# A narrower second token tile, chosen by a branch, in the experts of a hybrid attention and mixture-of-experts block

## The chip, the cores and the metric

The kernel runs on one core of one Trainium2 chip. The metric is device time of one execution in microseconds (us), the median of several runs; smaller is better. PE is the matrix engine, PEld its weight-load port, ACT the scalar engine, DVE the vector engine, POOL the general engine that issues the indexed transfers, SP the queue that issues plain ones.

## The reference

One encoder block over 1024 tokens of width 1024: a dilated and a two-dimensional neighbourhood attention, then a mixture of 16 experts in 4 groups, then a last normalisation. The change touches the experts alone:

```
g_idx  = top-1 group of each token             (4 groups)
e_idx  = top-2 experts inside that group       (4 experts each)
combine[token, expert] = softmax(two logits) * group weight
gate = x @ w_gate[e]      # 1024 -> 256
up   = x @ w_up[e]        # 1024 -> 256
act  = silu(gate) * up * combine[:, e]
out += act @ w_down[e]    # 256 -> 1024
```

The routing depends on the data. On the inputs of the reference the experts, in the order in which the kernel takes them, get 118, 118, 124, 137, 117, 132, 134, 205, 128, 59, 87, 172, 75, 99, 147 and 196 tokens. They are called e0 to e15 below. The products run in a split form: each float32 operand is a high part and a low part, and a product is the sum of high by high, high by low and low by high.

## The kernel before

The attention takes the first 624 us or so. The experts follow, in one loop over e0 to e13 (L1494 to L1553); e14 and e15 come in a tail after it.

For each expert the lists of its token numbers lie in `gi`. `gather` (L1357, an indexed transfer issued by POOL) brings up to 128 token rows into a tile `xg`. `tokens_in` (L1395) turns the tile by eight transposes on PE into two tiles, `x_hi` (written by ACT) and `x_lo` (written by DVE). `expert_up` (L1406) does 24 products of 128x512 into one PSUM bank: for each of 8 slices of the width `x_hi` by `g_hi`, `x_hi` by `g_lo`, `x_lo` by `g_hi`, where the 512 columns are gate and up side by side. ACT takes Silu of the gate half, DVE multiplies by the up half and by the token's weight into `act`. `act_in` (L1419) turns and splits `act`; `expert_down` (L1428) does 6 products for each half `z` of the 1024 outputs, and ACT evicts them into `ye`. `scatter` (L1455, an indexed transfer that adds into `acc_d` in device memory) puts `ye` back. In the rows a scatter with the index `idx` is that of an expert's last tile; one with the index `gi` is that of a first tile whose expert has a second one.

The down products of an expert run one turn of the loop later, among the gate and up products of the next, so that PE always has work. `split_up` and `split_down` split the next experts' weights in quarters on ACT (`g_hi`, `d_hi`) and DVE (`g_lo`, `d_lo`) between those.

An expert with more than 128 tokens has a second tile, gathered into `xg1`. Its work stands under a branch at L1527, which the four engines PE, ACT, DVE and POOL each take by a register loaded by `counts` (L1380) from the counts in `n_i`. In the branch stand, for the second tile, `tokens_in`, `expert_up`, and then the whole down step of the *first* tile (`expert_down` twice, into the PSUM tag `s`), its eviction into `y1` and its scatter; the second tile's own down step then takes the place of the first one's in the next turn. So with these counts the branch is taken at e3, e5, e6, e7 and e11, and jumped over at the nine others. An engine that jumps over it still does a wait for its own work and raises the semaphores that the branch would have raised; on POOL one such instruction is `INC_SWDGE_SEM`, for the indexed transfer's semaphore.

What sets the order: each engine runs its own instructions in the order of the code. The tile pools decide the waits: `ye` has two buffers, so an eviction into `ye` waits for the scatter of two evictions earlier to have landed. All scatters add into one tensor `acc_d`, and each waits for the landing of the one before it. The branch's own `ye` (L1531) is taken inside the branch.

Of the kernel before, what the change touches and what calls it, by code (L numbers as in the profile page):

```python
# [9 lines left out]
F32 = mybir.dt.float32  # L10
# [62 lines left out]
def build(nc, tc, a, ctx, dbg=None):  # L73
# [874 lines left out]
    pk = rt.tile([128, 2, 8], F32, name="pk")  # L948
    feat = rt.tile([128, 2, 8, 6, 16], BF, name="feat")
    C = rt.tile([128, 8, 16], BF, name="C")  # L950
    n_i = rt.tile([128, 17], I32, name="n_i")
    place = small[:, 0:32].rearrange("p (t e) -> p t e", t=8)
    token = small[:, 32:56].rearrange("p (t k) -> p t k", t=8)

# [398 lines left out]
    def at(e):  # L1353
        return slice(ORDER[e], ORDER[e] + 1)

    def gather(x, idx, src=hn_d):
        return nc.gpsimd.indirect_dma_start(out=x, out_offset=None, in_=src[:, :],  # L1357
                                            in_offset=bass.IndirectOffsetOnAxis(ap=idx, axis=0), bounds_check=1023,
                                            oob_is_err=False)

    def new_x(name="xg"):
        return ex.tile([128, 1024], F32, name=name, bufs=2)

    g_l = ex.tile([128, 1024], F32, name="g_l", bufs=1)
    bcast_row(g_l, a["norm_final_g"], 1024)
    x0 = {}
    for e in range(2):
        x0[e] = new_x()
        gather(x0[e], gi[:, 0, at(e)])

    cnt = pos[:, 16 * (8 - LAST):16 * (9 - LAST)]
    V.tensor_copy(n_i[:, 0:16], cnt)
    nmax = rt.tile([128, 1], F32, name="nmax")
    V.tensor_reduce(nmax, cnt, axis=X, op=ALU.max)
    V.tensor_copy(n_i[:, 16:17], nmax)
    ET = mybir.EngineType
    engines = (ET.PE, ET.Activation, ET.DVE, ET.Pool)

    def counts(c0, c1, which):
        return nc.values_load_multi_w_load_instructions(  # L1380
            n_i[0:1, c0:c1], engines=which, min_val=0, max_val=1024,
            skip_runtime_bounds_check_because="a count of tokens lies in 0..1024")[1]

    weights()
    n_val = counts(0, 16, engines)
    V.tensor_tensor(down0[1][:, 0], raw[:, 0], f(down0[0][:, 0]), op=ALU.subtract)
    down_raw[2] = load_down(2)
    up_raw[3] = [load_up(3, z) for z in range(2)]
# [6 lines left out]
    def tokens_in(x):  # L1395
        xh = ex.tile([128, 8, 128], F32R, name="x_hi")
        xl = ex.tile([128, 8, 128], F32R, name="x_lo")
        for q in range(2):
            pt = bank("pt")
            for k in range(4):  # L1400
                nc.tensor.transpose(pt[:, k * 128:(k + 1) * 128], x[:, (4 * q + k) * 128:(4 * q + k + 1) * 128],  # L1401
                                    ident)
            split(xh[:, 4 * q:4 * q + 4, :], xl[:, 4 * q:4 * q + 4, :], pt.rearrange("p (k t) -> p k t", k=4))
        return xh, xl

    def expert_up(xs, W, wcol, act):  # L1406
        gh, gl = W[0], W[1]
        xh, xl = xs
        ps = bank("mm")
        i = 0  # L1410
        for k in range(8):
            for l, wt in ((xh, gh), (xh, gl), (xl, gh)):
                nc.tensor.matmul(ps, l[:, k, :], wt[:, k, :], start=i == 0, stop=i == 23)  # L1413
                i += 1
        sg = ex.tile([128, 256], F32, name="sg", bufs=1)
        nc.scalar.activation(sg, ps[:, 0:256], AF.Silu)
        V.scalar_tensor_tensor(act, ps[:, 256:512], wcol, sg, op0=ALU.mult, op1=ALU.mult)

    def act_in(act):  # L1419
        pt = bank("s")  # L1420
        for k in range(2):
            nc.tensor.transpose(pt[:, k * 128:(k + 1) * 128], act[:, k * 128:(k + 1) * 128], ident)
        ah = ex.tile([128, 256], F32R, name="a_hi")
        al = ex.tile([128, 256], F32R, name="a_lo")
        split(ah, al, pt[:, 0:256])
        return ah, al

    def expert_down(aa, W, z, y=None, tag="o"):  # L1428

        ah, al = aa  # L1430
        dh, dl = W[2], W[3]
        c = slice(512 * z, 512 * z + 512)
        ps = bank(tag)
        i = 0
        for k in range(2):
            kk = slice(k * 128, (k + 1) * 128)
            for l, wt in ((ah, dh), (ah, dl), (al, dh)):
                nc.tensor.matmul(ps, l[:, kk], wt[:, k, c], start=i == 0, stop=i == 5)  # L1438
                i += 1
        if y is not None:  # L1440
            nc.scalar.activation(y[:, c], ps, AF.Copy)  # L1441
        return ps

    def new_y():
        return ex.tile([128, 1024], F32, name="ye", bufs=2)
# [2 lines left out]
        return ex.tile([128, 256], F32, name="act", bufs=2)  # L1448

    def second_gather(e):  # L1450
        x1[e] = new_x("xg1")
        gather(x1[e], gi[:, 1, at(e)])

    def scatter(d, idx, src, **kw):
# [13 lines left out]

    x1, xs, waiting, added = {}, {}, [], []
    spacer = ex.tile([128, 2], F32, name="spacer", bufs=1)[:, 0:1]

    def add_rows():
# [27 lines left out]
    for e in range(14):  # L1502
        if e:
            xs[e + 1] = tokens_in(x0.pop(e + 1))
            if e + 3 < 16:
                x0[e + 3] = new_x()
                gather(x0[e + 3], gi[:, 0, at(e + 3)])
        add_rows()
        if last:
            aa, before, y = act_in(last[0]), last, new_y()  # L1510
            W[e] = W[e] + split_down(down_raw.pop(e))
            down_raw[e + 2] = load_down(e + 2)
            W[e + 1], quarter = split_up(up_raw.pop(e + 1), (e + 1) % 2)
            for q in range(3):
                quarter(q)
        act = new_act()
        idx = ex.tile([128, 1], I32, name="idx", bufs=4)
        expert_up(xs.pop(e), W[e], ws[:, 0, at(e)], act)
        rows = [gi[:, q, at(e)] for q in range(2)]
        nc.gpsimd.tensor_copy(idx, rows[0])  # L1520
        if not last:
            xs[1] = tokens_in(x0.pop(1))
            x0[3] = new_x()
            gather(x0[3], gi[:, 0, at(3)])
        if last:
            expert_down(aa, W[e - 1], 0, y)
        with tc.If(n_val[ORDER[e]] > 128):  # L1527
            xs1 = tokens_in(x1.pop(e))
            aa1 = act_in(act)
            expert_up(xs1, W[e], ws[:, 1, at(e)], act)  # L1530
            y1 = new_y()  # L1531
            for z in range(2):
                expert_down(aa1, W[e], z, y1, tag="s")
            added.append((e, scatter(acc_d, rows[0], y1, compute_op=ALU.add)))
            nc.gpsimd.tensor_copy(idx, rows[1])
        if e:
            quarter(3)
        if 0 < e < 13:
            up_raw[e + 3] = [load_up(e + 3, z) for z in range(2)]
        if last:  # L1540
            expert_down(aa, W.pop(e - 1), 1, y)
            waiting.append((before[2], before[1], y))
        if e == 13:
            add_rows()
        if e + 2 < 14:
            second_gather(e + 2)
        elif e == 12:
            x1[e + 2] = new_x("xg1")
            gather(x1[e + 2], gi[:, 1, at(e + 2)])
        last = act, idx, e  # L1550
        if e == 2:
            kept_rows()
            n_top, = counts(16, 17, mybir.ALL_ENGINES)  # L1553
# [266 lines left out]
```

## Time and profile before

| | us |
|---|---|
| median of 3 runs | 895.49 (895.33 to 896.38) |
| the profiled execution, its own time | 894.3 |
| its span in the trace | 892.5 |
| PE busy in the span | 834.3 (93%) |
| PEld busy | 695.0 (78%) |
| DVE busy | 565.1 (63%) |
| ACT busy | 512.6 (57%) |
| POOL busy | 234.4 (26%) |

The mean granted clock of PE is 0.977 of full speed. The profiled execution's own time exceeds its span by 1.8 us, and lies 1.2 us under the median. The shares are means over the whole program; the stage of the experts runs from about 624 us to the end, and has other limits than the attention before it.

### The profile page before, as it was taken

To read this page: it belongs to the slowest core of one execution; us is meant where nothing else is said; L and a number is where in the kernel's file an instruction comes from. 1 tells how busy PE (TensorE), PEld (TensorE's weight loads), DVE (VectorE), ACT (ScalarE), POOL (GpSimd) and SP (SyncE) were. 2 spreads that over 40 slices of the span, in tenths; PEclk is the share of its full clock that TensorE was granted. 3 is DMA by queue.
4 is the path that set the end of the run, shared out by engine and by line. 5 is a ranking of instruction groups with operands and counts; after the bars stand their busy time and mean duration, and the time that the engine had idled before them with its cause. 6 is when DMAs were issued, how large, how long until landed. Compare 5 with 4: busy or idle time off the path is not lost. (4 is left out here: it accounts for less than half of the span.)

```text
span 892.5 us, 13330 instructions
## 1 busy us (share of the span) xinstructions
PE 834.3 (93%) x4492; PEld 695.0 (78%) x4492; DVE 565.1 (63%) x1255; ACT 512.6 (57%) x1082; POOL 234.4 (26%) x187
## 2 busy tenths in 40 slices
PE   8999999999999999999898999999799999999962
PEld 5888878979889888878787887887677877777741
DVE  4551126776767767666677754677786566858693
ACT  5441127757667576677576623543585665857652
POOL 4001122221232202332310100000443343734553
PEclk8999999999999999999999999998999999999985
DMA  6865452314344141534447747995798987999743
GB/s 238 278 217 162 126 160 65 100 52 108 94 138 105 53 138 48 148 103 117 79 157 206 254 154 248 360 323 213 250 317 248 293 233 226 361 299 304 217 180 129
DMA packets 129919, 167.30 MB, mean 187 GB/s; under 512 B 15222, under 2 KB 101750, under 8 KB 129824
## 3 DMA queue, kind: packets, MB, share of 16 engines
q1 hardware_dynamic: 119616, 142.53, 49.6%
q0 software_dynamic: 10224, 23.79, 9.8%
q8 instruction: 41, 0.67, 0.3%
q14 instruction: 38, 0.31, 0.1%
HBM read 129.93 MB, written 47.47 MB: 199 GB/s over the span
## 5 line engine op out<-in xcount | busy, mean ns | idle before, releaser
L103 ACT ACTIVATE pt_hi<-ps_pt 128x512 fp32r<-128x512 f32 (+2 forms) x128 | 67.6, 528 | 70.6 <-PE ps_pt L509 41.5
L378 PE MATMUL ps_mm<-xhi,w_lo 128*128 128x512 f32 x256 | 105.1, 411 | 1.1 <-POOL w_lo L104 1.1
L378 PE MATMUL ps_mm<-xlo,w_hi 128*128 128x512 f32 x256 | 105.0, 410 | 0.0
L378 PE MATMUL ps_mm<-xhi,w_hi 128*128 128x512 f32 x256 | 102.9, 403 | 0.0
L104 POOL TENSOR_TENSOR w_lo<-w_raw,w_hi 128x1024 fp32r<-128x1024 f32 x16 | 38.3, 2394 | 229.3 <-ACT w_hi L103 229.3
L104 DVE TENSOR_TENSOR pt_lo<-ps_pt,pt_hi 128x512 fp32r<-128x512 f32 (+2 forms) x128 | 77.2, 603 | 31.8 <-ACT pt_hi L103 31.2
L424 DVE CUSTOM_DVE_ANT_0 p<-ps_s,bias 128x256 f32<-128x256 f32 (+1 forms) x192 | 81.8, 450 | 18.2 <-PE ps_s L411 10.8
L104 DVE TENSOR_TENSOR g_lo<-raw_up,g_hi 128x1024 fp32r<-128x1024 f32 x64 | 75.4, 1220 | 24.6 <-ACT g_hi L103 24.6
L1413 PE MATMUL ps_mm<-g_hi,x_hi 128*128 128x512 f32 x184 | 75.4, 410 | 0.9 <-ACT x_hi L103 0.9
L1413 PE MATMUL ps_mm<-g_hi,x_lo 128*128 128x512 f32 x184 | 74.0, 402 | 1.8 <-DVE x_lo L104 1.8
L1357 POOL DMA_INDIRECT xg<-hn_d,gi x32 | 44.3, 1383 | 118.0 <-ACT ge L1078 81.7
L1413 PE MATMUL ps_mm<-g_lo,x_hi 128*128 128x512 f32 x184 | 73.3, 398 | 0.0
L430 ACT ACTIVATE p<-p,stats 128x256 f32<-128x256 f32 x128 | 63.7, 500 | 9.7 <-DVE stats L424 9.5
L103 ACT ACTIVATE g_hi<-raw_up 128x1024 fp32r<-128x1024 f32 x64 | 64.3, 1067 | 0.9
L411 PE MATMUL ps_s<-k_hh,q_s 128*128 128x256 f32 (+1 forms) x192 | 60.7, 324 | 4.3 <-DMA k_hh<-k_hh 1.7
L411 PE MATMUL ps_s<-k_low,q_s 128*128 128x256 f32 (+1 forms) x192 | 62.6, 334 | 0.0
L411 PEld LDWEIGHTS ps_s<-k_hh,q_s 128*128 128x128 f32 x192 | 44.6, 232 | 11.2 <-DVE q_s L402 2.6
L378 PEld LDWEIGHTS ps_mm<-xhi,w_lo 128*128 128x128 f32 x256 | 48.7, 190 | 5.2 <-POOL w_lo L104 1.4
L378 PEld LDWEIGHTS ps_mm<-xhi,w_hi 128*128 128x128 f32 x256 | 48.7, 190 | 3.2
L378 PEld LDWEIGHTS ps_mm<-xlo,w_hi 128*128 128x128 f32 x256 | 48.5, 189 | 3.5
L411 PEld LDWEIGHTS ps_s<-k_low,q_s 128*128 128x128 f32 x192 | 44.7, 233 | 3.5
L430 ACT ACTIVATE p<-p,nm 128x384 f32<-128x384 f32 (+1 forms) x64 | 37.5, 586 | 14.4 <-DVE nm L424 14.0
(307 smaller groups left out, 2152.8 us busy)
## 6 DMA issues: line engine op xcount, KB each, us to landing
raw_up<-in_w_gate SPq DMA_DIRECT2D x32, 512.0 KB
raw_up<-in_w_up SPq DMA_DIRECT2D x32, 512.0 KB
raw_down<-in_w_down SPq DMA_DIRECT2D x16, 1024.0 KB
w_raw<-in_w_in SPq DMA_DIRECT2D x16, 512.0 KB
xt<-in_x SPq DMA_DIRECT2D x8, 512.0 KB
k_hh<-in_w_in SPq DMA_DIRECT2D x8, 512.0 KB
va_d<-vt SPq DMA_DIRECT2D x16, 256.0 KB
vb_d<-vt SPq DMA_DIRECT2D x8, 512.0 KB
```

Of the source, the lines that this page charges most:

```text
L103: nc.scalar.activation(hi, src, AF.Copy)
L104: (nc.gpsimd if pool else nc.vector).tensor_tensor(lo, src, f(hi), op=ALU.subtract)
L378: nc.tensor.matmul(ps, l[:, k, :], x[half][:, k, :], start=i == 0, stop=i == 23)
L411: nc.tensor.matmul(ps, self.q[h][:, qs], keys(k[h]), start=n == 0, stop=n == 1)
L424: nc.vector.tensor_tensor_reduce(out=p, in0=ps, in1=bias, scale=-0.125, scalar=3.0e38, op0=ALU.add, op1=ALU.min, accum_out=nm)
L430: nc.scalar.activation(p, p, AF.Exp, bias=nm, scale=-1.0, accum_out=l)
L1357: return nc.gpsimd.indirect_dma_start(out=x, out_offset=None, in_=src[:, :], in_offset=bass.IndirectOffsetOnAxis(ap=idx, axis=0), bounds_c ...
L1413: nc.tensor.matmul(ps, l[:, k, :], wt[:, k, :], start=i == 0, stop=i == 23)
```

## The change

The `If` on more than 128 tokens becomes two in a row. The first, on more than 192 tokens, holds the old body. The second, on 129 to 192 tokens (a second tile of 1 to 64 tokens), holds the same steps with `few_tokens_in` and `few_up`. `few_tokens_in` writes the high parts of 64 tokens into columns 0 to 63 of one tile `x_hi`, and the low parts into columns 64 to 127. `few_up` then needs 16 products (this tile by `g_hi` and by `g_lo`, 8 slices each) where `expert_up` has 24; the result's rows 64 to 127 hold the low parts' share. ACT copies these rows into the spent token tile (`room`), DVE adds the two halves, and Silu and the weighting follow on 64 rows.

Around it: `n_i` gets 16 more columns, with two more DVE operations that fill them (the flag "129 to 192 tokens"); four engines load 16 more registers from them (`n_few`); `x0` of two experts and `x1` of two experts are cleared on POOL before they are first gathered into; `x1` of the first two is taken earlier; and `y1` is taken ahead of both branches.

```diff
-    n_i = rt.tile([128, 17], I32, name="n_i")
+    n_i = rt.tile([128, 33], I32, name="n_i")
...
-    x0 = {}
+
+    x0, x1 = {}, {}
     for e in range(2):
         x0[e] = new_x()
+        nc.gpsimd.memset(x0[e], 0.0)
+    for e in range(2):
         gather(x0[e], gi[:, 0, at(e)])
+    for e in range(2):
+        x1[e] = new_x("xg1")
+        nc.gpsimd.memset(x1[e], 0.0)
...
     V.tensor_copy(n_i[:, 16:17], nmax)
+
+    few = rt.tile([128, 16], F32, name="few")
+    V.tensor_scalar(few, cnt, 128.5, None, op0=ALU.is_gt)
+    V.scalar_tensor_tensor(n_i[:, 17:33], cnt, 192.5, few, op0=ALU.is_lt, op1=ALU.mult)
...
     n_val = counts(0, 16, engines)
+    n_few = counts(17, 33, engines)
...
+    def few_tokens_in(x):
+        xx = ex.tile([128, 8, 128], F32R, name="x_hi")
+        for q in range(2):
+            pt = bank("pt")
+            for k in range(4):
+                nc.tensor.transpose(pt[:, k * 128:(k + 1) * 128], x[:, (4 * q + k) * 128:(4 * q + k + 1) * 128],
+                                    ident)
+            ks = slice(4 * q, 4 * q + 4)
+            split(xx[:, ks, 0:64], xx[:, ks, 64:128], pt.rearrange("p (k t) -> p k t", k=4)[:, :, 0:64])
+        return xx, x
+
+    def few_up(xs, W, wcol, act):
+        xx, room = xs
+        ps = bank("mm")
+        i = 0
+        for k in range(8):
+            for wt in W[0:2]:
+                nc.tensor.matmul(ps, xx[:, k, :], wt[:, k, :], start=i == 0, stop=i == 15)
+                i += 1
+        few = slice(0, 64)
+        nc.scalar.activation(room[few, 0:512], ps[64:128, :], AF.Copy)
+        V.tensor_tensor(room[few, 512:1024], ps[few, :], room[few, 0:512], op=ALU.add)
+        sg = ex.tile([128, 256], F32, name="sg", bufs=1)
+        nc.scalar.activation(sg[few], room[few, 512:768], AF.Silu)
+        V.scalar_tensor_tensor(act[few], room[few, 768:1024], wcol[few], sg[few], op0=ALU.mult, op1=ALU.mult)
...
-        with tc.If(n_val[ORDER[e]] > 128):
-            xs1 = tokens_in(x1.pop(e))
-            aa1 = act_in(act)
-            expert_up(xs1, W[e], ws[:, 1, at(e)], act)
-            y1 = new_y()
-            for z in range(2):
-                expert_down(aa1, W[e], z, y1, tag="s")
-            added.append((e, scatter(acc_d, rows[0], y1, compute_op=ALU.add)))
-            nc.gpsimd.tensor_copy(idx, rows[1])
+        x, y1 = x1.pop(e), new_y()
+        for cond, tokens, up in ((n_val[ORDER[e]] > 192, tokens_in, expert_up),
+                                 (n_few[ORDER[e]] > 0, few_tokens_in, few_up)):
+            with tc.If(cond):
+                xs1 = tokens(x)
+                aa1 = act_in(act)
+                up(xs1, W[e], ws[:, 1, at(e)], act)
+                for z in range(2):
+                    expert_down(aa1, W[e], z, y1, tag="s")
+                added.append((e, scatter(acc_d, rows[0], y1, compute_op=ALU.add)))
+                nc.gpsimd.tensor_copy(idx, rows[1])
```

How the instructions stand on the engines shows in three places. The first is DVE where the counts become registers, just ahead of the first expert (`feat`, `part` belong to the routing, `d_lo` is the low part of the first down weights):

```order
 L1093 TENSOR_TENSOR feat<-ev,wb 128x8x48 x2
-L1380 TENSOR_LOAD n_i
-L1386 TENSOR_TENSOR d_lo<-raw_down,d_hi 128x1024
+L1390 TENSOR_LOAD n_i x2
+L1397 TENSOR_TENSOR d_lo<-raw_down,d_hi 128x1024
 L1144 COPY part<-ps_o 128x32
 L1145 TENSOR_TENSOR part<-part,ps_o 128x32
```

A second register load stands ahead of the low parts.

The second place is POOL around an expert's branch in the loop. Before (the instruction ISA is the `INC_SWDGE_SEM` of a branch that is jumped over; names such as Pool_49 are semaphores):

```order
L1520 COPY idx<-gi 128x1
L1527 COMPARE_AND_BRANCH
L1455 DMA acc_d<-ye,gi 1024x1024 [waits DMASW4_49,Activation_49]
L1535 COPY idx<-gi 128x1 [waits Pool_49]
L1527 UNCONDITIONAL_BRANCH
L1527 ISA [waits Pool_49,DMASW5_49]
L1527 UNCONDITIONAL_BRANCH
L1357 DMA xg_7927<-hn_d,gi 128x1024 [waits DMASW6_49,PE_49]
L1357 DMA xg<-hn_d,gi 128x1024 [waits DMASW7_49,PE_49]
L1455 DMA acc_d<-ye,idx 1024x1024 [waits DMASW4_49,DMASW5_49,Activation_49,Pool_49]
```

The same place after, from the first branch's jumped-over part on:

```order
L1569 ISA [waits Pool_49,DMASW6_49]
L1569 UNCONDITIONAL_BRANCH
L1569 COMPARE_AND_BRANCH
L1494 DMA acc_d<-ye,gi 1024x1024 [waits DMASW6_49,DMASW7_49,DMASW5_49,Activation_49]
L1576 COPY idx<-gi 128x1 [waits Pool_49]
L1569 UNCONDITIONAL_BRANCH
L1569 ISA [waits Pool_49,DMASW7_49]
L1569 UNCONDITIONAL_BRANCH
L1357 DMA xg_8181<-hn_d,gi 128x1024 [waits DVE_49,DMASW6_49,PE_49,Activation_49]
L1357 DMA xg<-hn_d,gi 128x1024 [waits DMASW7_49,PE_49]
L1494 DMA acc_d<-ye,idx 1024x1024 [waits DMASW6_49,DMASW5_49,DMASW7_49,Activation_49,Pool_49]
```

Each expert has two such branches in a row, each with its own copy of the jumped-over part, and the gather into `xg1` waits for DVE and ACT too, which now read and write that tile.

The third place is PE in the branch. Before, from the branch to the first products:

```order
L1527 COMPARE_AND_BRANCH
L1401 MATMUL ps_pt<-ident,xg_6711 128x128 x8
L1422 MATMUL ps_s<-ident,act 128x128 x2
L1413 MATMUL ps_mm<-g_hi,x_hi 128x512
L1413 MATMUL ps_mm<-g_lo,x_hi 128x512
L1413 MATMUL ps_mm<-g_hi,x_lo 128x512
```

In the narrow branch after:

```order
L1569 COMPARE_AND_BRANCH
L1436 MATMUL ps_pt<-ident,xg_7937 128x128 x8
L1460 MATMUL ps_s<-ident,act 128x128 x2
L1448 MATMUL ps_mm<-g_hi,x_hi 128x512
L1448 MATMUL ps_mm<-g_lo,x_hi 128x512
```

The product with `x_lo` is gone from each of the 8 slices.

## Rows read from the trace of the kernel before

**Rows 1.** Busy time by engine, e5's stretch (us, busy and count each, clock, DMA, GB/s).
```profile
692.00:712.00 20.00, 19.86 (x97) 15.92 (x96) 11.00 (x14) 11.61 (x20) 5.40 (x5) 1.00 0.97 317
```

**Rows 2.** Timeline of PE in e5's branch (start, us busy, engine, line, operation).
```profile
707.09 0.40 PE L1413 MATMUL ps_mm<-g_lo,x_hi 128*128 128x512 f32 x1
707.32 0.40 PE L1413 MATMUL ps_mm<-g_hi,x_lo 128*128 128x512 f32 x1
```

**Rows 3.** Start of the experts, and lines with clears and register loads (ns minimum/median/maximum).
```profile
L171 POOL MEMSET k_low<- x4: 944/945/950, 1.3 to 4.3; 64x1024 f32 x4
...
624.30 1.08 POOL L1357 DMA_INDIRECT xg<-hn_d,gi  x1 [81.67 <-ACT ge L1078]
...
L1380 DVEq TENSOR_LOAD <-n_i x2: 323/835/1347, 627.7 to 664.1; - x2
...
632.67 0.50 PE L1413 MATMUL ps_mm<-g_hi,x_lo 128*128 128x512 f32 x1 [1.76 <-DVE x_lo L104]
```

**Rows 4.** Timeline: DVE's smallest reduction by the counts, and PE around e2's jump.
```profile
623.27 0.16 DVE L1374 TENSOR_REDUCE nmax<-ps_pt 128x1 f32<-128x16 f32 x1
...
659.88 0.40 PE L1438 MATMUL ps_o<-d_hi,a_lo 128*128 128x512 f32 x1
660.42 0.47 PE L1438 MATMUL ps_o<-d_hi,a_hi 128*128 128x512 f32 x1
...
672.29 0.33 PE L1422 MATMUL ps_s<-ident,act 128*128 128x128 f32 x1 [1.28 <-DVE act L1417]
```

**Rows 5.** The branch's line: PE's 19 compares, POOL's nine semaphore raises (ns minimum/median/maximum).
```profile
L1527 PEldq COMPARE_BRANCH  x19: 70/179/342, 637.1 to 814.5; - x19
...
L1527 POOLq INC_SWDGE_SEM  x9: 460/965/1256, 640.8 to 822.1; - x9
```

**Rows 6.** Timeline of POOL, the scatters of e3 to e6.
```profile
682.01 1.59 POOL L1455 DMA_INDIRECT acc_d<-ye,gi  x1 [13.54 <-ACT ye L1441]
...
700.03 2.37 POOL L1455 DMA_INDIRECT acc_d<-ye,idx  x1 [4.15 <-ACT sg L1416]
...
711.39 1.58 POOL L1455 DMA_INDIRECT acc_d<-ye,gi  x1 [8.79 <-ACT ye L1441]
...
718.37 2.51 POOL L1455 DMA_INDIRECT acc_d<-ye,idx  x1 [1.46 <-ACT g_hi L103]
...
730.93 1.59 POOL L1455 DMA_INDIRECT acc_d<-ye,gi  x1 [9.84 <-ACT ye L1441]
```

**Rows 7.** Timeline of ACT, evictions into the branch's `ye` at e5, e6, e11.
```profile
709.71 0.60 ACT L1441 ACTIVATE ye<-ps_s 128x512 f32<-128x512 f32 x1 [1.52 <-DMA acc_d<-ye,idx]
...
728.69 0.60 ACT L1441 ACTIVATE ye<-ps_s 128x512 f32<-128x512 f32 x1 [0.96 <-PE ps_s L1438]
...
799.48 1.09 ACT L1441 ACTIVATE ye<-ps_s 128x512 f32<-128x512 f32 x2 [2.26 <-DMA acc_d<-ye,idx]
```

**Rows 8.** Landing times of the scatters issued at 718.37 and at 778.63.
```profile
DMA to landing us min/median/max: 10.2/10.2/10.2
...
DMA to landing us min/median/max: 10.7/10.7/10.7
```

**Rows 9.** Timeline of POOL from e8 to e11, where jumps follow one another.
```profile
758.68 2.39 POOL L1455 DMA_INDIRECT acc_d<-ye,idx  x1 [2.72 <-ACT sg L1416]
...
764.11 1.67 POOL L1357 DMA_INDIRECT xg<-hn_d,gi  x1 [1.98 <-DMA acc_d<-ye,gi]
...
768.31 2.57 POOL L1455 DMA_INDIRECT acc_d<-ye,idx  x1 [0.30 <-issue]
...
778.63 2.09 POOL L1455 DMA_INDIRECT acc_d<-ye,idx  x1 [0.78 <-issue]
...
790.21 1.60 POOL L1455 DMA_INDIRECT acc_d<-ye,idx  x1 [2.50 <-ACT ye L1441]
```

**Rows 10.** Timeline: last scatter of the loop on POOL, and the eviction after it.
```profile
819.04 1.79 POOL L1455 DMA_INDIRECT acc_d<-ye,idx  x1 [5.25 <-ACT sg L1416]
...
828.40 1.09 ACT L1441 ACTIVATE ye<-ps_o 128x512 f32<-128x512 f32 x2 [5.92 <-DMA acc_d<-ye,idx]
```

More of the change, by code (lines that the diff above doesn't have):

```diff
@@ L1450, in second_gather @@
     def second_gather(e):
-        x1[e] = new_x("xg1")
+        if e not in x1:
+            x1[e] = new_x("xg1")
         gather(x1[e], gi[:, 1, at(e)])
@@ L1467, in kept_rows @@
         V.tensor_copy(keep, t)
-    x1, xs, waiting, added = {}, {}, [], []
+    xs, waiting, added = {}, [], []
     spacer = ex.tile([128, 2], F32, name="spacer", bufs=1)[:, 0:1]
```

## The prediction

> **What bounds the kernel now.** I read first how busy each engine is in the experts' stretch, then the timelines of PE, ACT and POOL there, then what each waits for.
>
> In e5's stretch PE works 19.86 of 20 us [rows 1]. A reader who stops there says: PE is the bound, and a product that goes gives back its pitch. The pitch is 707.32 - 707.09 = 0.23 us [rows 2].
>
> The waits tell of a second bound that runs level with it: the chain of scatters. A scatter waits until the one before has landed, and the eviction into the branch's `ye` waits for the landing of the scatter issued at the start of the same turn. At e5 that scatter goes out at 700.03 [rows 6]; the eviction starts at 709.71, released by that transfer and not by PE [rows 7]; the branch's scatter follows at 711.39, the next at 718.37 [rows 6]. That one takes 10.2 us to land [rows 8], at 728.57, and e6's first eviction starts at 728.69 [rows 7]: PE and the transfer arrive together. At e11 the eviction waits 2.26 us for the transfer issued at 790.21 [rows 7, 9], and that one followed 778.63 + 10.7 = 789.33 [rows 8, 9]. In the tail an eviction waits 5.92 us for the scatter of 819.04 [rows 10].
>
> From e8 to e10, where three jumps follow one another, POOL itself sets the pace: the scatter at 768.31 comes 0.30 us after POOL's own last step, which is only issue; the one at 778.63 after 0.78, so 0.48 us of slack [rows 9]. A gather behind each jump starts after 1.98 us of idle time, released by the jump's semaphore raise [rows 9].
>
> So a product saved is worth its pitch only where PE, and not a landing, releases the next scatter.
>
> **The change part by part.**
>
> *The products.* By the counts e3, e5, e6 and e11 (129 to 192 tokens) take the narrow branch; e7, with 205, the old one. Each narrow branch has 8 products fewer, 8 x 0.2335 (the pitch before rounding) = 1.87 us; in all 7.5 us of PE's time.
> - e3: its branch's scatter at 682.01 waits for ACT's eviction only [rows 6]; no landing holds it. The full 1.87 is gained.
> - e5: the eviction can't start before the landing at 709.71. Two evictions back to back take 1.09 [rows 7], issue 0.30: scatter at 711.1 instead of 711.39, a gain of 0.3.
> - e6: its start scatter follows at 711.1 + 6.98 (718.37 - 711.39) = 718.1, lands at 728.3, and with 1.09 + 0.30 the branch's scatter goes at 729.7 instead of 730.93 [rows 6]: 1.2 in all for e5 and e6, where PE alone would give 3.7.
> - e11: the two evictions already run back to back behind the landing (1.09 for two) [rows 7]: nothing.
>
> So 1.87 + 1.2 = 3.1 of the 7.5 are reachable.
>
> *The narrow result's extra steps.* ACT's copy of 64x512, DVE's addition, Silu and the weighting stand in a row behind the last product. A 128x512 eviction takes 0.60 [rows 7]; at that price for each of the first three they take at most 1.8 us, under the 12 down products behind them (12 x 0.23 = 2.8). Without that cover it would be the 1.8, four times. I take nothing.
>
> *The clears.* A 64x1024 memset takes 0.95 on POOL [rows 3]; four full tiles are 4 such at up to twice that. POOL idles 81.67 us before the first gather [rows 3], and two clears fit there; the two of `x1` come behind the first gathers, before tiles that are read at e3 at the earliest. Nothing; without that cover up to 3.8. The `xg1` gather's new waits for DVE and ACT concern a tile last read two turns earlier: nothing.
>
> *The register load and the flags.* The earlier load of 16 registers takes 1.35 us on DVE (the larger of two) [rows 3], and stands ahead of the low parts which PE is waiting for: the product at 632.67 has waited 1.76 for `x_lo` [rows 3]. A second such load moves that start by 1.35, the two small DVE operations (0.16 each by a like one) [rows 4] by some 0.25: +1.6. Bounds: 1.0, if part of the load overlaps DVE's wait for its weights, and 2.5, if the load is preceded by semaphore waits of its own. I take 1.6, as DVE's chain from the load to `x_lo` has no gap that another engine sets.
> [...]
>
> *The jumps.* 23 jumps stand where 9 stood: one more at each of 14 experts. On PE a jump makes the pitch 660.42 - 659.88 = 0.54, so 0.31 more [rows 4], with compares of 0.07 to 0.34 [rows 5]. For e0 to e2 that is 0.9, of which 0.4 gets through, since e3's `act_in` waits 1.28 for DVE anyway [rows 4]; at e3 0.3; at e7 0.3; at the others the scatter chain covers it.
> On POOL, in e8 to e10, there is no cover. What a second jump costs right behind a first, no row shows. Ends: 0.46, the shortest semaphore raise alone [rows 5], and 1.98, the whole idle time of a first jump [rows 9], which includes the wait for the copy before it to drain. I take x = 1.25, the raise at its median of 0.97 [rows 5] and some 0.3 of issue.
>
> *The sum.* Start and e0 to e3: 1.6 + 0.4 + 0.3 - 1.87 = +0.4. e5 and e6: -1.2, so -0.8. e7: +0.3, so -0.5. The scatter behind e8's jump: +1.25, so +0.75. The one behind e9's: + 1.25 - 0.48, so +1.5. e10's jump lies under the 2.50 us that POOL waits before 790.21 [rows 9]. From there to the end the chain of landings carries the +1.5. On the profiled execution's own 894.3 that is 895.8; against the median of 895.49 it is **897.0**. The median lies 1.2 above that execution; all forecasts here are on the median's basis.
>
> **The rivals.**
> - *B, PE is the bound after all*: ACT's hold on the landing is hidden by work that PE has ready, and the change does what it says. -7.5 + 1.6 + 10 x 0.3 = -2.9: 892.6. For it: the 19.86 of 20. Against it: e5's and e11's evictions were released by a transfer while PE's result lay ready.
> - *C, POOL's second jump costs as much as the first*, x = 1.98: -0.5 + 1.98 + 1.98 - 0.48 = +3.0, 898.5, slower. It decides from x = 1.4 on. For it: each raise takes up to 1.26 [rows 5] and has its own drain. Against it: behind a jump nothing is left to drain.
> - *D, code loading*: each added jump lands on code not yet at hand. The row on PE speaks against it: nine jumps over the full body cost 0.31. At POOL's 1.98 for each of 14 it would be +28 at the worst; at half of that, on the path, some +14: 909.
> [...]
> - *E, the narrow branch is not taken*, if the counts in the registers differ from mine: the 3.1 are not gained: 897.0 + 3.1, less what hides, some 899.5.
>
> **How the numbers follow.** 0.2% (1.8 us) is about what a measurement of this kernel can tell from no change, so "same" is 893.7 to 897.3. A has 0.55; its own range, from x = 0.46 and a start of 1.6 (895.5) to x = 1.4 and a start of 2.2 (898.0), puts 0.43 in "same" and 0.12 in "slower". B 0.15 (0.14 faster, 0.01 same), C 0.20, D 0.05, E 0.05. Faster 0.14; same 0.44; slower 0.12 + 0.20 + 0.05 + 0.05 = 0.42. The range goes from B's 892.6 to 899.0, past C; outside lie half of B, D, and most of E: 0.07 + 0.05 + 0.04 = 0.16.
>
> **What would show it.** 19 x 8 = 152 products `g_hi` by `x_lo`, where 23 tiles made 184, and 2 x 32 products of the narrow form say that four narrow branches ran; the first product with `x_lo` at about 634.3 shows the start's term. e5's and e11's evictions still released by `acc_d`, with longer waits than 1.52 and 2.26, show that the chain swallowed the gain; PE idle there shows where it went. On POOL the idle time ahead of the gather behind a jump should be 1.98 + x, and the scatters of e8 to e10 further apart by x and x - 0.48. The forecast is wrong if those waits don't grow and the end moves down by 3 us, or if PE shows gaps far over 0.3 at jumps.

## The result, and the profile after

The changed kernel takes 902.6 us (median of 4 runs, 902.13 to 903.0) beside 895.41 of the kernel before: 1.010 of its time, interval 1.0080 to 1.0119. It is slower by 7.2 us by the medians and 9 by the ratio; the forecast was 897.0 and the range ended at 899.0. The profiled execution takes 902.44, with a span of 900.7.

The page's first part, of the kernel after: busy time, share of the span, instructions.

```profile
PE 828.0 (92%) x4460; PEld 690.0 (77%) x4460; DVE 571.0 (63%) x1261; ACT 515.5 (57%) x1086; POOL 238.7 (27%) x191
```

PE has 32 instructions fewer (4492 before), so the four narrow branches ran. It is busy 6.3 us less, and the span is 8.2 us longer.

Where the time went is read by holding the same instruction of both traces side by side, one profiled execution of each kernel. Both reach the routing's cast at L1087 at the same time (625.24 before, 625.18 after), so the starts below compare directly.

| place | before | after | shift, us |
|---|---|---|---|
| first product with `x_lo` | 632.67 | 638.55 | +5.9 |
| e0, last gate/up product | 639.22 | 645.50 | +6.3 |
| e1, last gate/up product | 648.64 | 656.83 | +8.2 |
| first product behind e1's jump | 650.58 | 659.15 | +8.6 |
| first product behind e2's jump | 660.42 | 669.48 | +9.1 |
| e3's branch, first product | 672.49 | 682.79 | +10.3 |
| e3's scatter | 682.01 | 690.50 | +8.5 |
| e6's scatter | 730.93 | 738.84 | +7.9 |
| scatter at the start of e8's turn | 758.68 | 766.73 | +8.1 |
| of e9's turn | 768.31 | 777.09 | +8.8 |
| of e10's turn | 778.63 | 788.39 | +9.8 |
| of e11's turn | 790.21 | 798.75 | +8.5 |
| last scatter of the loop | 819.04 | 827.73 | +8.7 |
| end of the span | 892.5 | 900.7 | +8.2 |

The whole loss stands ahead of e3's scatter. From there to the loop's last scatter the changed kernel loses 0.2 us, to the end of the span it gains 0.3. The first of these two is the better one to read. In the five traces in which the loop is that of the kernel before (its own, and those of e9, e10, e13 and e14 among the experiments below) the stretch from e3's scatter to the last scatter takes 136.7 to 137.4 us, but the stretch behind the loop takes anything from 72.8 to 76.1 us in the traces kept here, with the same code there (e8 and e11, which alter it, left out). A difference of 3 us at the end of one execution therefore tells nothing of the change.

The rows of the start, in the kernel after (timeline of DVE, POOL and PE: start, us busy, engine, line, operation, and in brackets the idle time before it and what ended that; the register loads with ns minimum/median/maximum over three loads). They answer to [rows 3]:

```profile
625.60 2.45 DVE L1089 CAST wb<-w 128x16 bf16<-128x16 f32 x1
626.15 1.85 POOL L1375 MEMSET xg<- 128x1024 f32 x2
628.08 0.17 DVE L1090 TENSOR_TENSOR w<-w,wb 128x16 f32<-128x16 f32 x1
...
L1390 DVEq TENSOR_LOAD <-n_i x3: 319/1356/3617, 629.8 to 672.9; - x3
...
635.00 1.23 DVE L1397 TENSOR_TENSOR d_lo<-raw_down,d_hi 128x1024 fp32r<-128x1024 f32 x1 [5.46 <-ACT g_hi L103]
...
638.55 0.80 PE L1424 MATMUL ps_mm<-g_hi,x_lo 128*128 128x512 f32 x1 [4.03 <-DVE x_lo L104]
639.15 0.63 PE L1424 MATMUL ps_mm<-g_hi,x_hi 128*128 128x512 f32 x1
639.58 0.63 PE L1424 MATMUL ps_mm<-g_lo,x_hi 128*128 128x512 f32 x1
```

Two things are to be seen. A cast of 128x16 takes 2.45 us; before, the same one took 0.24:

```profile
625.66 0.24 DVE L1089 CAST wb<-w 128x16 bf16<-128x16 f32 x1
```

It ends as the two clears of `x1` on POOL end (626.15 + 1.85 = 628.00). And of the two loads of 16 registers one takes 1.36 us and the other 3.62; the third, of one register, takes 0.32. Behind them DVE's 5.46 us of idle time ends at 635.00. The releaser that the profile names there is not what DVE waited for: from 629.8 it stood in the two loads, 1.36 + 3.62 = 4.98 us.

The last two rows show the third thing: 0.43 us from product to product instead of 0.23. PE's granted clock after and before, in stretches of 6 us (after the stretch its length; then busy us and count of PE, PEld, DVE, ACT and POOL; then the granted clock as a share of full speed, the DMA share and GB/s). After:

```profile
632.00:638.00 6.00, 2.48 (x14) 1.35 (x10) 2.94 (x6) 5.29 (x7) 3.80 (x4) 0.55 0.31 86
638.00:644.00 6.00, 5.45 (x15) 4.35 (x16) 5.63 (x6) 0.97 (x1) 0.00 (x0) 0.60 0.68 215
...
650.00:656.00 6.00, 6.00 (x22) 4.76 (x21) 5.80 (x7) 5.57 (x8) 2.78 (x3) 0.74 0.49 148
```

Before:

```profile
632.00:638.00 6.00, 5.33 (x16) 4.23 (x17) 5.75 (x7) 3.68 (x4) 3.22 (x3) 0.72 0.86 274
638.00:644.00 6.00, 4.32 (x29) 3.62 (x29) 2.26 (x4) 2.59 (x6) 2.51 (x3) 1.00 1.02 340
```

Both kernels have a stretch at half the full clock at the start: the granted clock is 0.50 from 633.5 to 636.5 before and from 633 to 642.5 after. The changed one has a longer pause of PE there (4.03 us before 638.55, inside this stretch, against 1.76 before 632.67, ahead of it), and a second such stretch at e1 (0.50 from 649.8 to 653), where the kernel before has none. In them a product of 512 columns comes every 0.426 us, which is 1.2 columns per ns; these are the stretches that the expectations below put at 1.2 GHz, while the traces give the clock as a share alone. What sets off the second stretch no run shows: other traces with two branches have one at e1 (e2 and e3, products of 0.61 to 0.64 us from 647.97 and 645.01) or at e3 (e7, 0.63 us from 674.08), and that of e4 has none there (products of 0.39 to 0.40 us from 642.09 on, up to 690).

At the jumps, PE after (idle time and releaser at the end):

```profile
659.15 0.47 PE L1476 MATMUL ps_o<-d_hi,a_hi 128*128 128x512 f32 x1 [0.56 <-PEq L1569]
669.48 0.47 PE L1476 MATMUL ps_o<-d_hi,a_hi 128*128 128x512 f32 x1 [0.66 <-PEq L1569]
681.18 1.06 PE L1436 MATMUL ps_pt<-ident,xg 128*128 128x128 f32 x8 [2.03 <-DVEq L1569]
682.79 0.51 PE L1448 MATMUL ps_mm<-g_hi,x_hi 128*128 128x512 f32 x1 [0.33 <-DVE x_hi L104]
```

Before, e3's transposes came without a wait:

```profile
669.97 1.04 PE L1401 MATMUL ps_pt<-ident,xg 128*128 128x128 f32 x8
```

Two jumps in a row make the pitch 0.95 (658.20 to 659.15) and 1.04 (668.44 to 669.48), where one made 0.55 and 0.54 ([rows 4] has the latter). The third row is a wait that the change makes: at e3 the narrow tile's transposes stand 2.03 us until DVE has arrived at the jump over the full branch: what the row names as the end of the wait is DVE's queue at L1569, the line of the branches.

The evictions into the branch's `ye` after, on ACT; they answer to [rows 7]:

```profile
717.94 0.60 ACT L1479 ACTIVATE ye<-ps_s 128x512 f32<-128x512 f32 x1
...
737.46 1.10 ACT L1479 ACTIVATE ye<-ps_s 128x512 f32<-128x512 f32 x2 [0.52 <-DMA acc_d<-ye,idx]
...
808.54 1.08 ACT L1479 ACTIVATE ye<-ps_s 128x512 f32<-128x512 f32 x2 [1.89 <-DMA acc_d<-ye,idx]
```

e6 and e11 are held by the landing of a scatter, e5 here is not.

On POOL, the first gather behind e8's jumps after; it answers to that of 764.11 in [rows 9]:

```profile
772.77 1.78 POOL L1357 DMA_INDIRECT xg<-hn_d,gi  x1 [3.30 <-DVE a_lo L104]
```

The idle time ahead of it is 3.30 us where it was 1.98; behind the jumps of e9 and e10 it is 3.70 and 3.58, where it was 2.01 and 2.06. Part of that is no loss, since POOL's steps ahead of it take less (scatter and copy 2.73, 2.76 and 2.85 us, before 3.45, 3.69 and 3.22): from the scatter to this gather it is 0.6, 0.8 and 1.2 us more than before (6.04 for 5.43 at e8).

### The profile page after: what moved, and what is told of

Its sections match the earlier page's. It is cut to its first block, busy times and chain, and to the rows that moved or that the text cites. A ratio compares the mean times of both kernels' runs of the same rounds, so it can differ in the third digit from the quotient of the medians.

```text
span 900.7 us, 13460 instructions
## 1 busy us (share of the span) xinstructions
PE 828.0 (92%) x4460; PEld 690.0 (77%) x4460; DVE 571.0 (63%) x1261; ACT 515.5 (57%) x1086; POOL 238.7 (27%) x191
## 5 line engine op out<-in xcount | busy, mean ns | idle before, releaser
L1424 PE MATMUL ps_mm<-g_hi,x_lo 128*128 128x512 f32 x152 | 61.4, 404 | 4.0 <-DVE x_lo L104 4.0
L1424 PE MATMUL ps_mm<-g_hi,x_hi 128*128 128x512 f32 x152 | 63.7, 419 | 0.0
L1424 PE MATMUL ps_mm<-g_lo,x_hi 128*128 128x512 f32 x152 | 61.8, 407 | 0.0
L442 DVE TENSOR_TENSOR ot<-ps_o,fold 64x512 f32<-64x512 f32 x36 | 30.9, 859 | 22.1 <-ACT fold L438 21.6
```

Source lines behind the costliest of these rows:

```text
L442: nc.vector.tensor_tensor(dst, view(ps[0:64, :]), view(t), op=ALU.add)
```

## The experiments

Each ratio is of a kernel's time to that of the kernel before, run on the same chip beside it; the interval is of 95%. Some differences below are given by the medians and some by the ratio, which need not agree to the microsecond; the interval belongs to the ratio.

**The start: e1_aligned, e2_noclear, e3_both.** In e1 the flags move one column:

```diff
-    V.tensor_copy(n_i[:, 16:17], nmax)
+    V.tensor_copy(n_i[:, 32:33], nmax)
...
-    V.scalar_tensor_tensor(n_i[:, 17:33], cnt, 192.5, few, op0=ALU.is_lt, op1=ALU.mult)
+    V.scalar_tensor_tensor(n_i[:, 16:32], cnt, 192.5, few, op0=ALU.is_lt, op1=ALU.mult)
...
-    n_few = counts(17, 33, engines)
+    n_few = counts(16, 32, engines)
```

> The changed kernel, with the 16 narrow flags in columns 16 to 31 of n_i instead of 17 to 32 (the maximum moves to column 32). Theory (place): the second register load is dear (3.62 us on DVE against 1.36 for the first, same 16 registers) because its first column lies 68 bytes into the row, so here it takes about 1.3 us; x_lo's first product comes 2.3 us earlier than 638.55 and the kernel takes 902.6 - 2.3 = 900.3, down to 899 if PE's shorter pause also spares it part of the stretch at 1.2 GHz. Rival (a second load is dear as such): it still takes some 3.6 us and the kernel 902.6.

e2 takes the clears away, e3 does both:

```diff
-        nc.gpsimd.memset(x0[e], 0.0)
...
-        nc.gpsimd.memset(x1[e], 0.0)
```

> The changed kernel without the four clears on POOL (nothing else). Theory (contention): DVE's cast that took 2.45 us beside the two clears of x1 (0.24 in the kernel before) goes back to 0.24, x_lo's first product comes 2.2 us earlier than 638.55, and the kernel takes 902.6 - 2.2 = 900.4, down to 899 with the clock. Rival (the cast was held by something else, such as the register loads beside it): the cast still takes about 2.4 us and the kernel 902.6.

> Both edits together: flags in columns 16 to 31, and no clears. Theory: the two add up, x_lo's first product at about 634.1 (the 632.67 of before, one load of 1.35 and the two flag operations more), the kernel at 902.6 - 4.5 = 898.1, or 896.5 if the second stretch at 1.2 GHz (7 products at e1, 1.5 us) goes too; what is left over the 895.4 of before is the 1.6 of the load and the jumps. Rival (the jumps and the chain of scatters cost most of the 7 us): the start moves, but the kernel stays above 900.5.

Measured: e1 900.94 us, ratio 1.0081 (1.0052 to 1.0111); e2 901.44, 1.0081 (1.0049 to 1.0112); e3 897.99, 1.0042 (1.0023 to 1.0060); before 894.40. In e1 the loads read

```profile
L1390 DVEq TENSOR_LOAD <-n_i x3: 310/1105/1355, 628.3 to 668.1; - x3
```

so the dear one is gone; in e2 the cast takes 0.18 us:

```profile
625.62 0.18 DVE L1089 CAST wb<-w 128x16 bf16<-128x16 f32 x1
```

Counted from the cast at L1087, `x_lo`'s first product comes at 7.43 us before, 13.37 in the changed kernel, 10.87 in e1, 11.25 in e2 and 8.72 in e3. In this row the two edits add up, 2.5 + 2.1 = 4.6. The whole kernel's time agrees with that for both together: the ratio falls from 1.010 to 1.0042, 5.2 us, and the intervals lie apart (by the medians, each against the kernel before on its own chip, 3.6 of 7.2 us come back). For one edit alone it can't tell: 1.0081 lies inside the changed kernel's interval. The rival of e3, over 900.5, is out. The clock's part did not come back in e3's profiled execution, which is the slowest of its seven: by the records of 0.60 to 0.64 us (0.39 to 0.40 at full clock), 18 products run at half the clock at e0 and e1, 15 in the changed kernel's and 8 before.

**One cause alone: e13_shift17, e14_shift4, e10_clears_only, e9_load_only.** These edit the kernel before.

```diff
-    V.tensor_copy(n_i[:, 0:16], cnt)
+    V.tensor_copy(n_i[:, 17:33], cnt)
...
-    n_val = counts(0, 16, engines)
+    n_val = counts(17, 33, engines)
```

> The kernel before with its one register load moved: the 16 counts stand in columns 17 to 32 of n_i (68 bytes into the row) instead of 0 to 15, the maximum in column 33. No other change. Theory (place): the load takes 3.6 us on DVE instead of 1.35, x_lo's first product comes 2.3 us later, and all of that reaches the end, with up to 1 us more at 1.2 GHz: 2.3 to 3.3 us over before. Rival (the dear one in the changed kernel was dear as the second, or by its registers' numbers): 1.35 us and no difference.

> The same with the counts in columns 4 to 19 (16 bytes into the row). It tells what place matters: if only a start inside the first 64 bytes or a multiple of 16 bytes is wanted, the load takes 1.35 us and the kernel as long as before; if the 16 values must not cross a multiple of 64 bytes, it takes 3.6 us and the kernel 2.3 to 3.3 us more, as e13.

> The kernel before with the four clears on POOL alone. Theory: DVE's small cast beside the second pair of clears takes 2.4 us instead of 0.24, x_lo comes 2.2 us later and so does the end: 2.2 us over before, to 3 with the clock. Rival (in this kernel DVE's register load comes at another time and the cast is not held): within 0.5 us of before.

e13: 897.58 us beside 894.29, ratio 1.0042 (1.0026 to 1.0058). e14: 895.91, 1.0018 (1.0002 to 1.0033). The load of e13 and that of e14:

```profile
L1380 DVEq TENSOR_LOAD <-n_i x2: 319/2088/3857, 625.9 to 664.9; - x2
```

```profile
L1380 DVEq TENSOR_LOAD <-n_i x2: 324/833/1342, 628.0 to 663.0; - x2
```

So it is the column: the one load there is takes 3.86 us when it starts 68 bytes into the tile's row, and 1.34 at 16 bytes, where the 16 values cross a multiple of 64 bytes. Of the four starts that ran (0, 16, 64 and 68 bytes) only the dear one is no multiple of 16; which finer step would do no run shows. The price of 2.5 us at the start reached the end (`x_lo` at 9.93 instead of 7.43; 3.3 us by the medians). The small difference of e14 has no row to it: its `x_lo` comes at 7.41.

e10: 897.08 beside 892.83, ratio 1.0045 (1.0027 to 1.0062). The cast held is another one, the next:

```profile
625.66 2.35 DVE L1091 CAST wb<-w 128x16 bf16<-128x16 f32 x1
626.11 1.85 POOL L1374 MEMSET xg<- 128x1024 f32 x2
```

`x_lo` comes at 9.54, 2.1 us later, and the kernel takes 4.2 us more by the medians, 2.4 to 5.5 by the interval: the clears that I had costed at nothing cost at least that 2.1. For what lies above it there is no row.

The held cast ends with the clears in both kernels (628.05 and 628.00 in the changed one, 628.01 and 627.96 in e10), and without them (e2) it takes 0.18; by the starts in the rows, though, it is the held cast that came first, 0.5 us ahead of the clears, when POOL was still at a gather. The gather alone does not hold it: before, the casts at 625.66 and 626.14 ran beside a gather of 625.69 to 626.71 and took 0.24 and 0.18. By what means clears on POOL hold a cast on DVE no row here shows.

e9 was to show the second load's price alone.

> The kernel before with the flags in columns 17 to 32 and the second register load alone; no branch uses it. Theory: the load takes 3.6 us on DVE, delays x_lo by 3.6 and the two flag operations, and since the experts run without slack behind it the whole of it reaches the end, with some 0 to 1.5 us of products at 1.2 GHz more: 3.6 to 5.1 us over before. Rival (a later wait, such as the landing of a scatter, takes part of the start's delay up again): under 2.5.

891.87 us beside 892.83, ratio 0.9981 (0.9963 to 1.0000). Its trace has no second load (two loads on each engine, of 1.35 and 0.33 us): nothing read the registers, and the load is not in the program that ran. It says nothing on the load. The two flag operations are there: from the cast into `n_i` to that of L1087 DVE takes 2.33 us where it took 2.05 before, so they cost DVE 0.28, ahead of the place from which the starts above are counted, and too little to show in the time of the kernel.

**The products and the jumps: e5_narrow_only, e6_jumps_only.** Both start from the kernel before. e5 puts the narrow body under the one branch:

```diff
         with tc.If(n_val[ORDER[e]] > 128):
-            xs1 = tokens_in(x1.pop(e))
+            xs1 = few_tokens_in(x1.pop(e))
             aa1 = act_in(act)
-            expert_up(xs1, W[e], ws[:, 1, at(e)], act)
+            few_up(xs1, W[e], ws[:, 1, at(e)], act)
```

> The kernel before with the narrow body under its one branch: no second branch, no second register load, no flags, no clears. e7 has 205 tokens, so 13 of its second tile's 77 are left out and their rows are wrong. It has five narrow tiles, 40 products fewer. Theory (the chain of scatters holds e5, e6 and e11): e3 gives its 1.87, e5 and e6 1.2 together, e7 no more than 1.2, e11 nothing: 3 to 4.3 us less than before. Rival (PE is the bound): 5 x 1.87 = 9.4 us less.

886.61 us beside 894.03, ratio 0.9927 (0.9905 to 0.9948): 6.5 us less by the ratio, 4.7 to 8.5. That is between the two theories, and outside the range of mine. The scatters of e3 and the last one of the loop (before: 682.01 and 819.04 [rows 6, 10]):

```profile
677.38 1.59 POOL L1481 DMA_INDIRECT acc_d<-ye,gi  x1 [12.93 <-ACT ye L1467]
...
809.72 2.21 POOL L1481 DMA_INDIRECT acc_d<-ye,idx  x1 [4.74 <-ACT sg L1416]
```

From the one to the other the profiled execution takes 132.3 us where the kernel before takes 137.0: e5, e6, e7 and e11 gave 4.7. Measured from e3's scatter, that of e6 comes 1.7 us earlier than before (1.2 expected for e5 and e6), that of e7 another 1.9 and the one at the start of e8's turn 1.2 more, 3.1 where I had allowed 1.2; e11 gave nothing more, as expected. So the miss is at e7, where PE and no landing released the scatter. With e3's own 1.9 this makes 6.6. Ahead of e3's scatter this execution gains 1.4 more, by the clock: its granted clock is 1.00 from 626 to 662, while the profiled one of the kernel before has 8 products at half the clock at e0, each 0.19 longer. ACT's waits at e5, e6, e7 and e11:

```profile
704.64 1.09 ACT L1467 ACTIVATE ye<-ps_s 128x512 f32<-128x512 f32 x2 [1.60 <-DMA acc_d<-ye,idx]
...
723.27 1.09 ACT L1467 ACTIVATE ye<-ps_s 128x512 f32<-128x512 f32 x2 [1.54 <-DMA acc_d<-ye,idx]
...
741.36 0.60 ACT L1467 ACTIVATE ye<-ps_s 128x512 f32<-128x512 f32 x1 [0.38 <-PE ps_s L1464]
...
790.59 1.09 ACT L1467 ACTIVATE ye<-ps_s 128x512 f32<-128x512 f32 x2 [2.55 <-DMA acc_d<-ye,idx]
```

e6 adds a second branch that is never taken:

```diff
-        with tc.If(n_val[ORDER[e]] > 128):
...
+        x, y1 = x1.pop(e), new_y()
+        for limit in (128, 1000):
+            with tc.If(n_val[ORDER[e]] > limit):
```

> The kernel before with a second branch behind the first, the same full body on more than 1000 tokens, which no expert has: 14 jumps more, everything else as before (one register load, 24 products, no clears). Theory (my sum's jump terms): 0.4 at e0 to e2, 0.3 at e3, 0.3 at e7, and 1.25 + 0.77 on POOL from e8 to e10: 3.0 us more than before. Rival (the jumps are hidden, POOL's too): within 0.5 us of before. Rival (code loading): over 5 us more.

897.77 us, ratio 1.0058 (1.0035 to 1.0080), 3.7 us more by the medians and 5.2 (3.1 to 7.2) by the ratio: the 14 jumps cost somewhat more than the 3.0 of my sum. Code loading at the price of rival D, 14 us, is out; the 5 us of the expectation are not. The figure is also not simply that of the changed kernel's jumps: here the added jump stands behind the taken body at e3, e5, e6, e7 and e11, there at e7 alone.

**The chain: e8_ye3, e11_narrow_ye3.** A third buffer for `ye`, without and with the narrow body (the gain's tile is cut to 128 columns and read eight times, to make room):

```diff
-        return ex.tile([128, 1024], F32, name="ye", bufs=2)
+        return ex.tile([128, 1024], F32, name="ye", bufs=3)
```

> The kernel before with three buffers for ye instead of two. To make room the last normalisation's gain is kept as 128 values and used eight times over, so the last product by it has wrong values in 7 of 8 column groups. An eviction into the branch's ye then no longer waits for the scatter issued at the start of the same turn. Theory: the waits of 1.52 (e5) and 2.26 (e11) on ACT and part of the tail's 5.92 go; e5 and e6 have PE as an equal bound, so they give little; 2 to 5 us less than before. Rival (the scatters themselves, each behind the landing of the one before, hold the end): within 1 us of before.

> e5_narrow_only with three buffers for ye (the gain of the last normalisation as in e8_ye3, and e7's rows past 192 tokens left out). In e5_narrow_only ACT waited 1.60, 1.54 and 2.55 us for a scatter to land before the evictions of e5, e6 and e11. Theory (these waits keep the rest of the products' gain): five tiles now give up to 9.4 us, and with the tail as in e8_ye3 the kernel takes 8 to 11 us less than before, 883 to 886. Rival (the scatters, each behind the landing of the last, keep it): 886.6 as without the third buffer, or 1 less.

e8: 891.54 beside 894.03, ratio 0.9982 (0.9968 to 0.9995), 0.4 to 2.9 us less, which decides neither for the theory nor for its rival. e11: 884.59 beside 892.83, ratio 0.9904 (0.9879 to 0.9928), 8.6 us less by the ratio. The waits on `acc_d` are gone from the branch's evictions; PE's results release them:

```profile
704.84 0.60 ACT L1471 ACTIVATE ye<-ps_s 128x512 f32<-128x512 f32 x1
705.81 0.60 ACT L1471 ACTIVATE ye<-ps_s 128x512 f32<-128x512 f32 x1 [0.38 <-PE ps_s L1468]
...
788.47 0.60 ACT L1471 ACTIVATE ye<-ps_s 128x512 f32<-128x512 f32 x1
```

From e3's scatter to e11's the kernel before takes 118.8 us and e5 114.6, so with two buffers the narrow body gains 4.3 there; with three, e8 takes 118.3 and e11 111.1, a gain of 7.2 of the 7.5 that four tiles save on PE. To the last scatter of the loop the gains are 4.7 (137.0 and 132.3) and 5.7 (136.4 and 130.7). The third buffer alone gives 0.5 and 0.6, about what executions of the same loop differ by (1.1 at e11's scatter, 0.7 at the last). So in these traces the landing of a scatter kept some 3 us of the products' gain up to e11, and some 1 us of it by the end of the loop. On the whole-kernel medians the step from e5 to e11 is not clear of the intervals.

**The order of the branches and the last load: e4_fewfirst, e7_codes, e12_codes_first.**

```diff
-        for cond, tokens, up in ((n_val[ORDER[e]] > 192, tokens_in, expert_up),
-                                 (n_few[ORDER[e]] > 0, few_tokens_in, few_up)):
+        for cond, tokens, up in ((n_few[ORDER[e]] > 0, few_tokens_in, few_up),
+                                 (n_val[ORDER[e]] > 192, tokens_in, expert_up)):
```

> The changed kernel with the narrow branch ahead of the full one. In the changed kernel the narrow branch's transposes wait for DVE to arrive at the jump over the full branch (2.03 us at e3, 4.4 in all for three). Theory: with the narrow branch first this wait is gone at e3, e5, e6, e11 and appears at e7 alone; since at e5, e6 and e11 the chain of scatters holds anyway, the end gains the 1.3 to 2 of e3 only: 901. Rival (these waits set the end at each of the four): 902.6 - 4.4 = 898.2.

902.07 us, ratio 1.0093 (1.0063 to 1.0123): not to be told from the changed kernel. The rival's 4.4 us are out; whether the 1.3 to 2 of e3 are there can't be told.

e7 keeps one load, of a code:

```diff
-    V.tensor_copy(n_i[:, 0:16], cnt)
+    V.tensor_scalar(over, cnt, 192.5, None, op0=ALU.is_gt)
+    V.scalar_tensor_tensor(n_i[:, 0:16], cnt, 128.5, over, op0=ALU.is_gt, op1=ALU.add)
...
-    n_few = counts(17, 33, engines)
...
+        for cond, tokens, up in ((n_val[ORDER[e]] > 1, tokens_in, expert_up),
+                                 (n_val[ORDER[e]] == 1, few_tokens_in, few_up)):
```

> The changed kernel without the clears and without the second register load: one load of 16 codes (0, 1 for 129 to 192 tokens, 2 for more), and the two branches test the code. Against e3_both it saves the second load of 1.35 us. Theory: 1.35 less than e3_both, or up to 2.5 with a shorter stretch at 1.2 GHz: 0.5 to 2.3 us over before, since jumps of 3 stand against 3.1 of products. Rival (the second load was covered): no less than e3_both, 3.6 over before.

> e7_codes with the narrow branch ahead of the full one. There PE waited 1.99, 1.10 and 1.09 us at e3, e5 and e11 for DVE to arrive at the jump over the full branch before the narrow tile's transposes. Theory: at e3 the 2 us come back in full, at e5 and e11 the scatter landing holds the eviction anyway; the second jump behind the narrow body puts 1 to 1.5 us before the next scatter instead: 0.5 to 1.5 us less than e7_codes, 894.6 to 895.6. Rival: the jump costs as much behind the body as ahead of it, no difference.

e7: 896.08 beside 894.03, ratio 1.0039 (1.0024 to 1.0055). The start is as before (`x_lo` at 7.61), and still the kernel is slower than before; beside e3 (1.0042) the saved load of 1.35, 0.15%, can't be told from nothing. e12: 897.70 beside 892.83, ratio 1.0040 (1.0025 to 1.0055), not to be told from e7. The traces show a price behind the body. POOL around e3 in e7, and then in e12:

```profile
682.64 1.59 POOL L1490 DMA_INDIRECT acc_d<-ye,gi  x1 [13.55 <-ACT ye L1475]
...
684.76 1.08 POOL L1357 DMA_INDIRECT xg<-hn_d,gi  x1 [0.15 <-ACT x_hi L103]
```

```profile
681.21 1.59 POOL L1490 DMA_INDIRECT acc_d<-ye,gi  x1 [12.98 <-ACTq L1565]
...
685.14 1.98 POOL L1357 DMA_INDIRECT xg<-hn_d,gi  x1 [1.72 <-DVE a_lo L104]
```

With the narrow branch first the gather behind it comes 3.93 us after the scatter instead of 2.12, and the next scatter 8.5 us after it instead of 6.9: of what PE no longer waits for at e3, POOL pays 1.6 us behind the body.

No complete version of the change beat the kernel before.

## Why the prediction was wrong, point by point

The step that failed is the start, "+1.6" for the load and the flags and "nothing" for the clears: the first product with `x_lo` came 5.9 us later, by 3.6 of the load and 2.2 of the clears, and by e3's scatter the sum's +0.4 stood at +8.5.

- *The register load* (+1.35 and 0.25 taken, bounds 1.0 to 2.5): mis-sized, and the bound too low. The load took 3.62 us. I took the row of the load of 16 registers as the price of another load of 16, and did not look at where it starts in its row; e1, e13 and e14 show that the place decides (1.10 to 1.36 us at 0, 16 and 64 bytes, 3.6 to 3.9 at 68). The flags cost the 0.25 that I took (0.28 on DVE, e9).
- *The clears* ("nothing"): wrong. I checked that POOL was idle and not what else ran beside it. The two clears of `x1` on POOL held a cast of DVE for 2.2 us, and DVE is the engine that PE waits for there (e2, e10). My bound without cover, 3.8, spoke of POOL's time, the wrong engine.
- *The clock*: not in the sum at all. In the profiled execution PE's longer pause came with a longer stretch at half the clock: 0.4 us at e0 (+5.9 to +6.3), and a second stretch cost some 1.5 at e1 (its products take from 649.93 to 656.83, 6.9 us, against 5.4).
- *The jumps on PE at e0 to e2* (0.9, of which 0.4): 1.3 us in the table (0.5 at e0, 0.4 at e1, 0.5 at e2).
- *e3* (0.3 - 1.87): the products gave their 1.8, from +10.3 to +8.5, and the narrow result's extra steps cost nothing there, as taken. The branch's start cost 1.2, not 0.3: PE waits 2.03 us for DVE to arrive at the jump, a wait that the order of PE alone does not show. I had DVE's 1.28 us wait as cover; it is the same engine that now has the jump to do.
- *e3 to the end* (+1.1 by the sum): +0.2 at the last scatter of the loop, -0.3 at the end. e5 and e6 gave 0.6 (-1.2 forecast); e8 to e10 cost 0.7 and 1.0 (1.25 and 0.77); e11's turn gave 1.2 back, where POOL had 2.50 us of idle time [rows 9] and my sum carried everything through. That this half came out near is in part luck: the sum gave e5 and e6 0.6 too much and e11's turn 1.2 too little, and the two runs that price products and jumps apart both lay above their forecasts (e5 with 6.5 for 3 to 4.3, the surplus at e7, which is not narrow in the change; e6 with 5.2 for 3.0). The reason that I gave for the products' lost gain, the landing of the scatters, is there (e5, e11), but it keeps less than I said by the end of the loop.
- *The signs that I named*: the waits at e5's and e11's evictions did not grow (e5's is gone, e11's is 1.89 for 2.26, and e6 has one of 0.52); why e5's went, no run shows. The idle time on POOL behind a jump did grow, by 1.3 to 1.7 us where I had put x = 1.25, but from scatter to gather only by 0.6 to 1.2.
- *The rivals*: C's mechanism (POOL's second jump) was there, at somewhat less than my middle price. B, by which each product gives its pitch, fell with e5 (6.5 of 9.4 us), D's price with e6 (5.2 us for 14 jumps), E by the count of products; whether any part of a jump's price is the loading of code no run shows.

In one line: the steps from e3's scatter on came out within 1.5 us, in part by errors that cancel; the steps ahead of it were priced as if every engine had its own time there, and missed 8 us, 5.9 of them before the first product with `x_lo`.

How much of the remaining 0.4% of e7 lies at e0 to e2, and how much at the narrow branch's waits, I did not separate by a run. A version with one branch inside the other, that would jump over both at once, was not run.

## What to carry to other kernels

An idle engine is cover only if what it does there takes nothing from an engine that is waited for: look at what runs beside the place, not at the engine's own gap (here two clears on an idle POOL, beside which a cast on DVE took 2.45 us instead of 0.24). Two instructions of the same name and size need not have one price if their operands lie differently (here two loads of 16 registers, 1.36 and 3.62 us); where the start of a load changes, take a range. And a gain on the busiest engine is read from who releases the next step: here landings kept 3 us of it up to e11, and second jumps took 0.4 to 0.5 us of PE each, with a wait of 2.03 us for DVE at e3.

## What the runs showed of the hardware

- A load of 16 registers on DVE takes 1.34 to 1.36 us from byte 0 or 16 of the tile's row, 1.10 or 1.36 from byte 64 (e1 has two loads, from 0 and from 64; its rows do not say which takes which), and 3.6 to 3.9 us from byte 68 (before, after, e1, e13, e14).
- A DVE cast of 128x16 to bf16 takes 0.18 to 0.34 us with no clear beside it, and 2.35 to 2.45 beside two POOL clears of 128x1024, where it ends 0.05 us after them (after, e2, e7, e10).
- Two jumps in a row cost PE 0.4 to 0.5 us more than one (0.95 for 0.55 at e1, 1.04 for 0.54 at e2). The second raise of semaphores on POOL takes about as long as the first, and both grow from turn to turn (after: 23 of them, 0.47 and 0.43 us at e0, 1.27 and 1.26 at e13).
